# Layer 1 of a two-layer diffusion backbone: v normalised by ScalarE, gates issued behind weight halves, and a rearranged last product

## The chip, the cores and the metric

The kernel runs on one core of a Trainium2 chip. Its time is the device time of one execution in microseconds (us); several runs are made and their median is given. The engines are TensorE (PE, with PEld for its weight loads), VectorE (DVE), ScalarE (ACT), GpSimd (POOL) and SyncE (SP), which only issues transfers here.

## The reference

The model has two layers over 512 latent tokens (width 1024) and 256 context tokens. Layer 0 is a bidirectional retention mixer, and the change leaves it alone. Layer 1, on the latent tokens, is a chunked gMLP:

```
u = h @ w_in[:, :2048];  v = h @ w_in[:, 2048:4096];  z = h @ w_in[:, 4096:]
v = v - mean(v);  v = v * rsqrt(mean(v * v) + eps) * vnorm_g      # per token
mixed = einsum('gij,bnjgc->bnigc', w_s, v in chunks of 128 tokens) + b_s
y = u * mixed
out = (y * silu(z)) @ w_out
x = x + gate * out;   result = rmsnorm(x, final_g)
```

The mean and the square mean run over all 2048 features of a token, so v has to be complete before one value of it can be normalised. Everything is float32; the matmuls are made of three products of a rounded high part and a low part.

## The kernel before, in words

**High and low parts.** Each weight tile of 128 x 1024 is loaded raw by SP, then split: ACT casts it to the high part (`CAST hl<-raw`), DVE subtracts that from the raw tile for the low part (`TENSOR_TENSOR hl<-raw,hl`, called the low below). `mm3` (line 109) issues the three products. One helper (line 54) records every PE, ACT and DVE instruction, so the profile names line 54 for all of them and the tile names tell them apart.

**Seven products for eight.** u and z of layer 1 are made in eight units (i = 0 to 7). A unit takes four raw tiles, named 11, 12, 22 and 21, and forms seven products of a Strassen-like scheme in the order `SINGLE = ("B11", "T1", "T2", "B21", "T3", "B22", "T4")`. A T product first needs a difference of two raw tiles (`TENSOR_TENSOR raw<-raw` on DVE), then cast and low. Each product is 24 matmuls of 256 columns. The four results are 11, 12, 22 and 21; ACT copies (`COPY snap<-pst`) and DVE sums (`TENSOR_TENSOR snap<-pst,snap`) take the first three out of PSUM, the last stays there. B11, T2, T3 and T4 add into one PSUM bank (`Product.run`), so the copy after T2 has to be over before T3 writes.

**Weight halves ahead.** `Q.get()` (class `Stream`, line 137) hands out the next split tile and writes the splitting of the tiles up to two further on into the program. Split tiles live in four rotating buffers (`hl`), raw tiles in seven slots, other temporaries in eleven rotating buffers (`t2`: `snap`, `vt`, `ya`, `yz`, `xs`). SP issues transfers in order; one whose slot is still read holds up those behind it.

**v.** v was made before the units and stored in DRAM as `vt`, one block of 256 features per unit. `load_vt` (line 1266) brings a block back as two tiles and DVE normalises each 128 x 256 piece in place, four per unit. After B22 of a unit 16 small matmuls (`pst<-wsT,vt`) mix the tokens of that block: two banks, one for each of the two feature tiles 2i and 2i+1.

**Gates.** `gate_f` (line 1276) makes y of one feature tile: silu(z) on ACT (`yz`), mixed times norm gain plus bias (`SCALAR_TENSOR_TENSOR ya<-pst,sv,bsb`), two multiplications by u, one by silu(z), then cast and low. Feature tile 2i+1 takes results 12 and 22, feature tile 2i takes 11 and 21, the last of which comes with T4. The first is written behind B22, the second behind T4.

**Last product.** `out1(p)` (line 1211), p = 0 to 3, multiplies four y tiles by the output weights; p = 0, 1, 2 follow units 2, 4, 6, and p = 3 follows unit 7. It works on two column halves (hf) of 512, for each on four row tiles t of 128 tokens, and k runs over the four y tiles; p = 3 ends in `final`, the last RMSNorm and the store of the rows. For p = 3, hf = 0 the y tiles k = 0, 1, 3 come first for each t, and k = 2 (feature tile 14, which waits for T4) last.

**Order.** PE works in the order of the text. In this part of the program ACT, DVE and SP are free within data dependencies: a scheduler of the language sets their order when the program is built, so the order on each engine is fixed but not that of the text.

Of the kernel before, what the change touches and what calls it, by code (L numbers as in the profile page):

```python
# [9 lines left out]
AF = mybir.ActivationFunctionType  # L10
ALU = mybir.AluOpType
AX = mybir.AxisListType

P = 128
D = 1024
# [4 lines left out]
NT = SEQ // P  # L20
# [6 lines left out]
HS = 256  # L27
# [40 lines left out]
def hybrid_kernel(ctx, tc, xT_d, cT_d, cv_d, sv_d, rows_d, ada0_d, adag_d, w_d, rope_d, dec_d, ws_d, id_d, out_d):  # L68
    nc = tc.nc
    pe, act, dve = (Queue(tc, e) for e in (nc.tensor, nc.scalar, nc.vector))  # L70
# [11 lines left out]
    def st(shape, tag, dt=F32, bufs=1, name=None):  # L82
        return sb.tile(shape, dt, tag=tag, name=name or tag, bufs=bufs)

    T2 = 11
# [15 lines left out]
    def t2(name, shape=(P, 512), dt=F32):  # L101
        return st(list(shape), "t2", dt, bufs=T2, name=name)

    def pt(shape=(P, 512), tag="ps"):
        return ps.tile(list(shape), F32, tag=tag, name="pst", bufs=6 if tag == "ps" else 2)
# [3 lines left out]
    def mm3(out, l, r, first, last):  # L109
        (lh, ll), (rh, rl) = l, r  # L110
        mm(out, ll, rh, start=first, stop=False, skip_group_check=True)
        mm(out, lh, rl, start=False, stop=False, skip_group_check=True)
        mm(out, lh, rh, start=False, stop=last, skip_group_check=True)

    def split(hl, src, late=None):
        h, l = hl
        act.copy(h, src)
        low = lambda: dve.tensor_tensor(l, src, f32(h), ALU.subtract)
        if late is None:
            low()  # L120
        else:
            late.append(low)
# [4 lines left out]
    def load(dst, src):  # L127
        nc.sync.dma_start(dst, src)  # L128
# [83 lines left out]
    Q = Stream()  # L212
# [62 lines left out]
    UZ = 8  # L275
# [918 lines left out]
    fg = st([P, D], "g0", name="fg")  # L1194
    load(fg, rows_d[1:2, :].partition_broadcast(P))

    mv = st([P, NT, 2], "mv")
    for t in range(NT):
        dve.bn_aggr(mv[:, t, :], bns[:, t, :, :])
    rv = st([P, NT], "rv")  # L1200
# [3 lines left out]
    o1 = [st([P, D], f"s{t}", name="o1") for t in range(NT)]  # L1204
# [3 lines left out]
    def yf(f):  # L1208
        return ys[f % 6]

    def out1(p):
        for hf in range(2):
            ws = [Q.get() for _ in range(2)]
            pr = {}
            if p == 3 and hf == 0:
                seq = [(t, k) for ks in ((0, 1, 3), (2,)) for t in range(NT) for k in ks]
            else:
                seq = [(t, k) for t in range(NT) for k in range(4)]
            ends = (2,) if p == 3 and hf == 0 else (3,)
            for t, k in seq:  # L1220
                if k == 0:
                    pr[t] = pt()
                y = yf(4 * p + k)
                w = ws[k // 2][:, :, k % 2 * 512:k % 2 * 512 + 512]
                mm3(pr[t], (y[:, 0, t * P:t * P + P], y[:, 1, t * P:t * P + P]), (w[:, 0, :], w[:, 1, :]), k == 0, k in ends)
                if k in ends:
                    drain(p, t, hf, pr.pop(t))

    def drain(p, t, hf, pr):
        h = slice(hf * 512, hf * 512 + 512)  # L1230
        s = o1[t][:, h]
        if p == 0:
            act.copy(s, pr)
            return
        dve.tensor_tensor(s, pr, s, ALU.add)
        if p == 2:
            xs = t2("xs")
            load(xs, x1_d[2 * t + hf])
            dve.tensor_tensor(s, s, Q.gate[:, h], ALU.mult)
            dve.tensor_tensor(s, s, xs, ALU.add)  # L1240
        if p == 3:
            final(t, hf, s, h)

    ends = {}

    def final(t, hf, s, h):
        if hf == 0:
            ends[t] = (st([P, 2], "fss", bufs=4), st([P, D], f"w{t}", name="o"))
        ss, o = ends[t]
        act.activation(t2("junk1"), s, AF.Square, accum_out=ss[:, hf:hf + 1])  # L1250
        if hf == 0:
            dve.tensor_scalar(ss[:, 0:1], ss[:, 0:1], 1.0 / D, EPS, ALU.mult, ALU.add)
        dve.tensor_tensor(o[:, h], s, fg[:, h], ALU.mult)
        if hf == 0:
            return
        rows = out_d[t * P:t * P + P, :]
        act.activation(ss[:, 1:2], ss[:, 1:2], AF.Sqrt, bias=ss[:, 0:1], scale=1.0 / D)
        dve.reciprocal(ss[:, 1:2], ss[:, 1:2])
        dve.tensor_scalar(o[:, 0:512], o[:, 0:512], ss[:, 1:2], None, ALU.mult)
        load(rows[:, 0:512], o[:, 0:512])  # L1260
        act.activation(o[:, 512:], o[:, 512:], AF.Copy, scale=ss[:, 1:2])
        load(rows[:, 512:], o[:, 512:])

    vts = {}

    def load_vt(i):
        vts[i] = []
        for th in range(2):
            v = t2("vt", (P, 2, HS))
            load(v, vt_d[i][:, 2 * th:2 * th + 2, :])  # L1270
            for t in range(2):
                n = 2 * th + t
                dve.tensor_scalar(v[:, t, :], v[:, t, :], mv[:, n, 0:1], rv[:, n:n + 1], ALU.subtract, ALU.mult)
            vts[i].append(v)

    def gate_f(f, pm, mine):

        g = f // 2
        a = t2("ya")
        z1 = t2("yz")  # L1280
        bb = bsb[:, g * P:g * P + P].unsqueeze(1).to_broadcast([P, NT, P])
        for th in range(2):
            act.activation(z1[:, th * HS:th * HS + HS], mine[th][:, HS:], AF.Silu)
        dve.scalar_tensor_tensor(a.rearrange("p (n i) -> p n i", n=NT), pm.rearrange("p (n i) -> p n i", n=NT),
                                 vg[:, f:f + 1], bb, ALU.mult, ALU.add)
        for th in range(2):
            h = a[:, th * HS:th * HS + HS]
            dve.tensor_tensor(h, mine[th][:, 0:HS], h, ALU.mult)
        dve.tensor_tensor(a, a, z1, ALU.mult)
        y = yf(f)  # L1290
        split((y[:, 0, :], y[:, 1, :]), a)

    load_vt(0)
    for i in range(UZ):
        got, pms = {}, {}
        prod = Product(features, got.__setitem__)
        for name in SINGLE:
            prod.run(name, Q.get())
            if name == "T2" and i < UZ - 1:
                load_vt(i + 1)  # L1300
            if name == "B22":
                for s in range(2):
                    pm = pms[s] = pt()
                    for n in range(NT):
                        mm(pm[:, n * P:n * P + P], vts[i][n // 2][:, n % 2, s * P:s * P + P], wsT[:, i * P:i * P + P], start=True, stop=True)
                gate_f(2 * i + 1, pms[1], {0: got["12"], 1: got["22"]})
        gate_f(2 * i, pms[0], {0: got["11"], 1: got["21"]})
        if i and i % 2 == 0:
            out1(i // 2 - 1)
    out1(3)  # L1310


# [108 lines left out]
```

## Time and profile before

| what | value |
|---|---|
| median of 3 runs | 913.14 us (909.51 to 913.16) |
| profiled execution | 911.76 us |
| its span, first to last instruction | 910.0 us |
| PE busy | 886.6 us (97%) |
| DVE busy | 722.4 us (79%) |
| ACT busy | 445.5 us (49%) |
| clock granted to TensorE, mean | 0.997 |

A timeline row gives the start in us, the length in us, the engine, the line, the instruction with its tiles and shape, how many it merges (x24), and in brackets the idle time ahead of it on that engine with what ended it. A row of grouped instructions gives the count, the busy time, the mean length in ns, and the idle time ahead. Instructions of one engine overlap a little, so a merged row is shorter than the count times the mean.

Units 0 to 7 begin on PE at 635.72 us; the last matmul ends at about 903.7 us.

### The profile page before, as it was taken

How to read it: one execution, taken by the hardware profiler on the slowest of the kernel's cores; microseconds unless marked ns; L12 is line 12 of the kernel's file. 1: busy time of each engine (PE TensorE's matmuls, PEld its weight loads, DVE VectorE, ACT ScalarE, POOL GpSimd, SP SyncE). 2: the span in 40 equal slices, each digit the busy share in tenths (PEclk: the TensorE clock that was granted, in tenths of full speed). 3: DMA queues.
4: the chain of work that ended last, by engine and by line, in shares of the span. 5: the costliest groups of instructions: out<-in, count | busy, mean ns of one | idle time of the engine just before them, and what ended most of it. 6: DMA issues, size and time to landing. Idle time of an engine off the chain costs nothing.

```text
span 910.0 us, 16953 instructions
## 1 busy us (share of the span) xinstructions
PE 886.6 (97%) x6872; PEld 840.4 (92%) x6872; DVE 722.4 (79%) x1024; ACT 445.5 (49%) x683; POOL 51.5 (6%) x88
## 2 busy tenths in 40 slices
PE   8999999999999999999999999999999999999987
PEld 6899999999999998998989798999999899899885
DVE  3689978698789866888666759999899479679985
ACT  5565644434545436626362548744546445244244
POOL 0001211101102010000000001111000000000000
PEclk9999999999999999999999999999999999999999
DMA  9943968556667377758163611626335035037102
GB/s 334 389 136 111 308 200 255 163 183 223 211 207 241 107 254 251 257 164 282 43 194 107 200 37 66 200 102 220 129 116 185 24 116 185 24 117 253 49 24 93
DMA packets 76782, 153.81 MB, mean 169 GB/s; under 512 B 7840, under 2 KB 34592, under 8 KB 76704
## 3 DMA queue, kind: packets, MB, share of 16 engines
q1 hardware_dynamic: 69840, 130.70, 44.5%
q0 software_dynamic: 6720, 22.03, 6.3%
q8 instruction: 54, 0.88, 0.4%
q14 instruction: 24, 0.20, 0.1%
q10 hardware_dynamic: 144, 0.01, 0.0%
HBM read 128.58 MB, written 24.12 MB: 168 GB/s over the span
## 4 chain that ended last, share of the span: by engine, by line
PE 61%; DVE 20%; DMA 7%; ACT 5%; issue 5%; SPq 1%; DVEq 0%; ACTq 0%
PE pst L54 61%; DVE hl L54 5%; DMA raw<-in_w_dram 4%; DVE raw L54 4%; DVE ya L54 2%; ACT hl L54 2%; DVE o L54 2%; DMA vt<-vt 2%; SPq L128 1%; DMA acc<-in_xT_dram 1%; DVE pf L54 1%; DMA xq<-in_xT_dram 1%; DVE snap L54 1%; DVE ada_a L54 1%; ACT junk L54 1%
## 5 line engine op out<-in xcount | busy, mean ns | idle before, releaser
L54 DVE TENSOR_TENSOR hl<-raw,hl 128x1024 fp32r<-128x1024 f32 x195 | 236.7, 1222 | 65.5 <-ACT hl L54 64.8
L54 ACT CAST hl<-raw 128x1024 fp32r<-128x1024 f32 x195 | 202.7, 1049 | 140.9 <-DVE raw L54 71.1
L54 PE MATMUL pst<-oS,hl 128*128 128x256 f32 x1104 | 135.6, 280 | 4.3 <-DVE hl L54 3.7
L54 PEld LDWEIGHTS pst<-oS,hl 128*128 128x128 f32 x1104 | 131.4, 188 | 6.6 <-ACT ya L54 3.6
L54 PE MATMUL pst<-hl,oS 128*128 128x256 f32 x1152 | 137.3, 279 | 0.1
L54 PEld LDWEIGHTS pst<-hl,oS 128*128 128x128 f32 x1152 | 135.6, 188 | 1.2 <-ACT snap L54 0.8
L54 PE MATMUL pst<-oA,hl 128*128 128x256 f32 x936 | 118.1, 281 | 0.2
L54 PEld LDWEIGHTS pst<-oA,hl 128*128 128x128 f32 x936 | 112.6, 188 | 2.6 <-DVE raw L54 0.8
L54 DVE TENSOR_TENSOR raw<-raw 128x1024 f32<-128x1024 f32 x92 | 111.5, 1221 | 0.8
L54 PE MATMUL pst<-hl,oA 128*128 128x256 f32 x816 | 99.4, 280 | 0.1
L54 ACT COPY snap<-pst 128x512 f32<-128x512 f32 x92 | 53.9, 586 | 89.4 <-PE pst L54 89.1
L54 PEld LDWEIGHTS pst<-hl,oA 128*128 128x128 f32 x816 | 96.9, 188 | 0.4 <-issue 0.3
L54 PE MATMUL pst<-og,hl 128*128 128x256 f32 x768 | 93.1, 281 | 0.0
L54 PEld LDWEIGHTS pst<-og,hl 128*128 128x128 f32 x768 | 91.2, 188 | 1.0 <-issue 0.5
L54 PE MATMUL pst<-hl,ya 128*128 128x512 f32 x288 | 69.6, 394 | 2.4 <-DVE ya L54 2.4
L54 PEld LDWEIGHTS pst<-hl,ya 128*128 128x128 f32 x288 | 53.9, 188 | 14.7 <-DVE ya L54 2.9
L54 PE MATMUL pst<-v,ph 128*128 128x512 f32 x192 | 60.9, 399 | 0.0
L54 DVE TENSOR_TENSOR snap<-pst,snap 128x512 f32<-128x512 f32 x69 | 47.4, 687 | 4.1 <-PE pst L54 3.9
L54 ACT CAST ph<-pf 128x512 fp32r<-128x512 f32 x24 | 14.9, 621 | 70.9 <-DVE pf L54 68.5
L54 PE MATMUL pst<-hl,hc 128*128 128x256 f32 x384 | 47.5, 279 | 0.0
L54 PEld LDWEIGHTS pst<-hl,hc 128*128 128x128 f32 x384 | 45.9, 188 | 0.0
L54 PEld LDWEIGHTS pst<-v,ph 128*128 128x128 f32 x192 | 36.7, 191 | 7.7
(172 smaller groups left out, 971.8 us busy)
## 6 DMA issues: line engine op xcount, KB each, us to landing
raw<-in_w_dram SPq DMA_DIRECT2D x224, 256.0 KB, 4.5
bg<-in_adag_dram SPq DMA_DIRECT2D x32, 512.0 KB, 4.4
ada_w<-in_ada_dram SPq DMA_DIRECT2D x16, 512.0 KB, 9.0
raw<-in_w_dram SPq DMA_DIRECT2D x16, 512.0 KB, 4.4
bg<-in_dec_dram SPq DMA_DIRECT2D x12, 512.0 KB, 4.3
v<-snap POOLq DMA_DIRECT2D x16, 256.0 KB, 5.1
z<-snap POOLq DMA_DIRECT2D x16, 256.0 KB, 4.7
v<-v SPq DMA_DIRECT2D x8, 512.0 KB, 4.2
```

Of the source, the lines that this page charges most:

```text
L54: made = op(*args, **kw)
L128: nc.sync.dma_start(dst, src)
```

## The change

Four edits, all in layer 1:

- v is normalised by ACT: y = rv * v + nb with nb = -mean * rv, a 128 x 4 tile made once by DVE (`ACTIVATE vt<-vt,nb,rv`), where DVE had subtracted and multiplied. The block for the next unit is now loaded after T1 (it was T2), and its normalisation is written after T4.
- A gate isn't written at once but put on a list (`owed`). `settle`, called after the next `Q.get()`, first pins the DVE order at that point (`fence`: later DVE instructions stay behind the one recorded last) and then writes the gates that are owed. In unit 7 the second gate is written at once.
- In the last product, hf = 0: k = 0 and 1 for all row tiles, then k = 3 for all, then k = 2 for all.
- In the last product, hf = 1: the last row tile is made in two column pieces of 256 (`last`), each with its own sum of squares; the last store is issued by ACT's queue instead of SP's.

```
             ws = [Q.get() for _ in range(2)]
             pr = {}
+            settle()
             if p == 3 and hf == 0:
-                seq = [(t, k) for ks in ((0, 1, 3), (2,)) for t in range(NT) for k in ks]
+                seq = [(t, k) for ks in ((0, 1), (3,), (2,)) for t in range(NT) for k in ks]
...
+                if (p, hf, t) == (3, 1, NT - 1):
+                    continue
...
+            if (p, hf) == (3, 1):
+                t = NT - 1
+                for c in range(2):
+                    pq = pt((P, HS))
+                    for k in range(4):
+                        y = yf(4 * p + k)
+                        o = k % 2 * 512 + c * HS
+                        w = ws[k // 2][:, :, o:o + HS]
+                        mm3(pq, (y[:, 0, t * P:t * P + P], y[:, 1, t * P:t * P + P]), (w[:, 0, :], w[:, 1, :]), k == 0, k == 3)
+                    last(t, c, pq)
...
+    def last(t, c, pq):
+        h = slice(512 + c * HS, 512 + c * HS + HS)
+        s = o1[t][:, h]
+        dve.tensor_tensor(s, pq, s, ALU.add)
+        ss, o = ends[t]
+        act.activation(t2("junk1", (P, HS)), s, AF.Square, accum_out=ss[:, 1:2])
+        dve.tensor_tensor(o[:, h], s, fg[:, h], ALU.mult)
+        if c == 0:
+            dve.scalar_tensor_tensor(ss[:, 0:1], ss[:, 1:2], 1.0 / D, ss[:, 0:1], ALU.mult, ALU.add)
+            return
...
+        act.activation(o[:, 512:], o[:, 512:], AF.Copy, scale=ss[:, 1:2])
+        nc.scalar.dma_start(rows[:, 512:], o[:, 512:])
...
             load(v, vt_d[i][:, 2 * th:2 * th + 2, :])
-            for t in range(2):
-                n = 2 * th + t
-                dve.tensor_scalar(v[:, t, :], v[:, t, :], mv[:, n, 0:1], rv[:, n:n + 1], ALU.subtract, ALU.mult)
             vts[i].append(v)
+    nb = st([P, NT], "nb")
+    dve.scalar_tensor_tensor(nb, mv[:, :, 0], -1.0, rv, ALU.mult, ALU.mult)
+    def norm_vt(i):
+        for n in range(NT):
+            v = vts[i][n // 2][:, n % 2, :]
+            act.activation(v, v, AF.Identity, bias=nb[:, n:n + 1], scale=rv[:, n:n + 1])
+    owed = []
+    def settle():
+        if owed:
+            dve.fence()
+        while owed:
+            owed.pop(0)()
...
     load_vt(0)
+    norm_vt(0)
     for i in range(UZ):
...
         for name in SINGLE:
-            prod.run(name, Q.get())
-            if name == "T2" and i < UZ - 1:
-                load_vt(i + 1)
+            w = Q.get()
+            settle()
+            prod.run(name, w)
+            if i < UZ - 1:
+                if name == "T1":
+                    load_vt(i + 1)
+                if name == "T4":
+                    norm_vt(i + 1)
...
-                gate_f(2 * i + 1, pms[1], {0: got["12"], 1: got["22"]})
-        gate_f(2 * i, pms[0], {0: got["11"], 1: got["21"]})
+                owed.append(lambda f=2 * i + 1, pm=pms[1], mine={0: got["12"], 1: got["22"]}: gate_f(f, pm, mine))
+        owed.append(lambda f=2 * i, pm=pms[0], mine={0: got["11"], 1: got["21"]}: gate_f(f, pm, mine))
+        if i == UZ - 1:
+            settle()
```

How the instructions move is shown at three places; numbers behind names are those of buffers and differ between the two programs. First DVE, where unit 1 ends and the T2 tile of unit 2 is made. Before, `ya_7951` is the gate of feature tile 3, `ya_7989` that of feature tile 2, and `hl_8000<-raw_7594` is the low of the T2 tile:

```order
L54 SCALAR_TENSOR_TENSOR ya_7951<-pst_7946,sv_95,bsb_7460 128x512
L54 SCALAR_TENSOR_TENSOR ya_7989<-pst_7941,sv_95,bsb_7460 128x512
L54 TENSOR_TENSOR ya_7951<-snap_7836,ya_7951 128x256
L54 TENSOR_TENSOR ya_7951<-snap_7803,ya_7951 128x256
L54 TENSOR_TENSOR ya_7989<-snap_7773,ya_7989 128x256
L54 TENSOR_TENSOR ya_7951<-ya_7951,yz_7952 128x512
L54 TENSOR_TENSOR ya_7989<-pst_7748,ya_7989 128x256
L54 TENSOR_TENSOR raw_7594<-raw_7630,raw_7594 128x1024
L54 TENSOR_TENSOR ya_7478<-ya_7951,ya_7478 128x512
L54 TENSOR_TENSOR ya_7989<-ya_7989,yz_7990 128x512
L54 TENSOR_TENSOR hl_8000<-raw_7594,hl_8000 128x1024
L54 TENSOR_TENSOR ya_7478<-ya_7989,ya_7478 128x512
```

The same place in the changed program, where `ya_7953` is feature tile 3, `ya_7995` feature tile 2, and `hl_7992<-raw_7592` the low of the T2 tile; `hl_8032` is the low of B21, the product after it:

```order
L54 TENSOR_TENSOR raw_7592<-raw_7628,raw_7592 128x1024
L54 SCALAR_TENSOR_TENSOR ya_7953<-pst_7944,sv_95,bsb_7460 128x512
L54 TENSOR_TENSOR ya_7953<-snap_7842,ya_7953 128x256
L54 TENSOR_TENSOR ya_7953<-snap_7805,ya_7953 128x256
L54 TENSOR_TENSOR hl_7992<-raw_7592,hl_7992 128x1024
L54 TENSOR_TENSOR ya_7953<-ya_7953,yz_7954 128x512
L54 SCALAR_TENSOR_TENSOR ya_7995<-pst_7939,sv_95,bsb_7460 128x512
L54 TENSOR_TENSOR hl_8032<-raw_7815,hl_8032 128x1024
L54 TENSOR_TENSOR ya_7478<-ya_7953,ya_7478 128x512
L54 TENSOR_TENSOR ya_7995<-snap_7775,ya_7995 128x256
L54 TENSOR_TENSOR ya_7995<-pst_7750,ya_7995 128x256
```

Before, seven gate instructions stood ahead of the raw difference for T2 (`raw<-raw`) and two more between it and its low; now there are three between the two, none ahead, and the rest of the gates follows behind the low.

Second ACT in unit 1, where the block of v for unit 2 (`vt_7807`, `vt_7809`) is normalised. `snap_7842` is the copy out of PSUM after T2, which T3 waits for. Before:

```order
L54 COPY snap_7773<-pst_7748 128x512
L54 CAST ya_7478<-ya_7734 128x512
L54 CAST hl_7775<-raw_7554 128x1024
L54 CAST hl_7806<-raw_7297 128x1024
L54 COPY snap_7803<-pst_7778 128x512
L54 CAST hl_7846<-raw_7300 128x1024
L54 COPY snap_7836<-pst_7748 128x512
L54 CAST hl_7879<-raw_7554 128x1024
```

and in the changed program (`snap_7836` above is `snap_7842` here):

```order
L54 COPY snap_7775<-pst_7750 128x512
L54 CAST hl_7812<-raw_7297 128x1024
L54 CAST ya_7478<-ya_7740 128x512
L54 COPY snap_7805<-pst_7780 128x512
L54 CAST hl_7844<-raw_7300 128x1024
L54 ACTIVATE vt_7807<-vt_7807,nb_7481,rv_7471 128x256
L54 COPY snap_7842<-pst_7750 128x512
L54 CAST hl_7877<-raw_7560 128x1024
L54 ACTIVATE vt_7807<-vt_7807,nb_7481,rv_7471 128x256
L54 ACTIVATE vt_7809<-vt_7809,nb_7481,rv_7471 128x256 x2
```

The first normalisation stands ahead of the copy after T2, so that copy also waits for the transfer of `vt_7807`. The same happens in units 4 and 6; in units 0, 2, 3 and 5 the copy comes first.

Third PE, the end of the program: the last product, one piece of the difference.

```order
 L54 MATMUL pst<-wsT,vt 128x128 x8
 L54 MATMUL pst<-oA_6831,hl 128x256 x24
-L54 MATMUL pst<-hl,ya 128x512 x96
-L1417 UNCONDITIONAL_BRANCH
+L54 MATMUL pst<-hl,ya 128x512 x84
+L54 MATMUL pst<-hl,ya 128x256 x24
+L1470 UNCONDITIONAL_BRANCH
```

Twelve matmuls of 512 columns became 24 of 256.

More of the change, by code (lines that the diff above doesn't have):

```diff
@@ L1262, in final @@
         load(rows[:, 512:], o[:, 512:])
+    def last(t, c, pq):
[8 more added lines that the diff above has]
+            return
+        rows = out_d[t * P:t * P + P, :]
+        act.activation(ss[:, 1:2], ss[:, 1:2], AF.Sqrt, bias=ss[:, 0:1], scale=1.0 / D)
+        dve.reciprocal(ss[:, 1:2], ss[:, 1:2])
+        dve.tensor_scalar(o[:, 0:512], o[:, 0:512], ss[:, 1:2], None, ALU.mult)
+        load(rows[:, 0:512], o[:, 0:512])
+        act.activation(o[:, 512:], o[:, 512:], AF.Copy, scale=ss[:, 1:2])
+        nc.scalar.dma_start(rows[:, 512:], o[:, 512:])
     vts = {}
```

## The prediction

> **What bounds the kernel now.** I read the page's shares first, then TensorE's timeline over layer 1, then DVE's timeline at one of TensorE's gaps, and last the end of the program. The page:
>
> ```profile
> span 910.0 us, 16953 instructions
> PE 886.6 (97%) x6872; PEld 840.4 (92%) x6872; DVE 722.4 (79%) x1024; ACT 445.5 (49%) x683; POOL 51.5 (6%) x88
> ```
>
> TensorE is busy for 97%, and the change takes no matmul work away. It can only gain where TensorE stands still behind 635 us, and behind the last matmul. TensorE's timeline of units 0 to 7 has five gaps:
>
> ```profile
> 663.90 3.04 PE L54 MATMUL pst<-oS,hl 128*128 128x256 f32 x24 [0.94 <-DVE hl L54]
> 687.21 3.04 PE L54 MATMUL pst<-oS,hl 128*128 128x256 f32 x24 [1.60 <-DVE hl L54]
> 690.09 2.96 PE L54 MATMUL pst<-oA,hl 128*128 128x256 f32 x24
> 752.82 3.04 PE L54 MATMUL pst<-oS,hl 128*128 128x256 f32 x24 [0.56 <-DVE hl L54]
> 819.02 3.04 PE L54 MATMUL pst<-oS,hl 128*128 128x256 f32 x24 [0.62 <-DVE hl L54]
> 878.84 1.56 PE L54 MATMUL pst<-hl,ya 128*128 128x512 f32 x6
> 882.83 20.88 PE L54 MATMUL pst<-hl,ya 128*128 128x512 f32 x90 [2.43 <-DVE ya L54]
> ```
>
> The first four are T2 of units 1, 2, 4 and 6, each waiting for a low; they sum to 0.94 + 1.60 + 0.56 + 0.62 = 3.72 us. The fifth is the last product waiting for a y tile, 2.43 us. What lies ahead of the largest of the four, on DVE:
>
> ```profile
> 680.20 1.40 DVE L54 SCALAR_TENSOR_TENSOR ya<-pst,sv,bsb 128x512 f32<-128x512 f32 x2
> 681.51 1.08 DVE L54 TENSOR_TENSOR ya<-snap,ya 128x256 f32<-128x256 f32 x3
> 682.52 0.69 DVE L54 TENSOR_TENSOR ya<-ya,yz 128x512 f32<-128x512 f32 x1
> 683.12 0.42 DVE L54 TENSOR_TENSOR ya<-pst,ya 128x256 f32<-128x256 f32 x1
> 683.45 1.22 DVE L54 TENSOR_TENSOR raw<-raw 128x1024 f32<-128x1024 f32 x1
> 684.59 0.69 DVE L54 TENSOR_TENSOR ya<-ya 128x512 fp32r<-128x512 f32 x1
> 685.19 0.69 DVE L54 TENSOR_TENSOR ya<-ya,yz 128x512 f32<-128x512 f32 x1
> 685.84 1.23 DVE L54 TENSOR_TENSOR hl<-raw,hl 128x1024 fp32r<-128x1024 f32 x1
> ```
>
> DVE has no idle time here: two gates run, and the low that TensorE waits for ends at 687.07. In units 0 and 1 DVE is close to full, 18.80 of 20 us:
>
> ```profile
> 680.00:700.00 20.00, 18.40 (x158) 18.23 (x157) 18.80 (x27) 11.48 (x15) 0.00 (x0) 1.00 0.43 136
> 840.00:860.00 20.00, 20.00 (x98) 16.69 (x97) 20.00 (x30) 3.73 (x5) 0.00 (x0) 1.00 0.24 91
> ```
>
> (columns: stretch, length, busy PE, PEld, DVE, ACT, POOL, granted clock, transfer share, GB/s). ACT has room in both.
>
> **The change part by part.** First v on ACT. What DVE loses and ACT gains:
>
> ```profile
> L54 DVE TENSOR_SCALAR vt<-vt,mv,rv 128x256 f32<-128x256 f32 x32 | 11.5, 411 | 11.1 <-DMA vt<-vt 11.0
> L54 ACT ACTIVATE f<-f,sh,gs 128x256 f32<-128x256 f32 x16 | 8.3, 592 | 1.1 <-DVE f L54 1.1
> L54 ACT ACTIVATE yz<-snap 128x256 f32<-128x256 f32 x24 | 9.2, 413 | 27.5 <-DVE snap L54 27.4
> ```
>
> DVE is rid of 11.5 us of work and of 11.1 us spent standing behind `vt` transfers, 2.8 us a unit. The new ACT instruction is the form of the second row, an earlier scaling with a column of scales and one of shifts: 0.59 us; the nearest cheaper row, 0.41, is the lower end. ACT gains 32 x 0.59 = 18.9 us (13.2 by the lower end), 2.4 a unit, and in units 0 and 1 it is busy for 11.48 of 20 us. No part of this is on TensorE's path by itself. [...]
>
> Second the gates behind weight halves. Ahead of the low at 685.84 the new order leaves one `SCALAR_TENSOR_TENSOR` (half of 1.31), two `ya<-snap` (two thirds of 1.01) and the raw difference; the other gate work, from 680.20 to 685.84 without the raw difference 4.50 us, shrinks to 0.66 + 0.67 = 1.33. So the low comes 3.2 us earlier by the order alone, and by up to 2.8 us more from v: twice and more the largest gap of 1.60. I take all four gaps as gone, **3.72 us**; the lower bound is 0, where the raw tiles and not DVE set the time (rival A). What becomes late instead is the second gate of each unit. Its y tile is needed at the earliest after the next unit but for the last product, and its two PSUM banks return six allocations later, so nothing waits for it up to unit 6.
>
> At unit 7 there is a cost. The second gate of unit 6 now lies between the row sums of the last but one product, where the second windows row shows DVE at 20.00 of 20 us. T2's raw difference of unit 7 now stands behind nearly all those sums. Counting the new order from the end of unit 6's T4 with the lengths above and 0.6 us for each 512-column row operation, its low ends some 0.3 us after T2 could start. I take **-0.3 us**, with 0 to -1.
>
> Third the order of the last product. Six matmuls took 878.84 to 880.24; now the 24 of k = 0 and 1 take 4 x 1.40 = 5.6 us, so tile 15 is needed at 884.4 and tile 14 at 884.4 + 2.8 = 887.2. In the profile the lows of both ended by 883.4:
>
> ```profile
> 879.89 0.42 DVE L54 TENSOR_TENSOR ya<-pst,ya 128x256 f32<-128x256 f32 x1
> 880.95 1.22 DVE L54 TENSOR_TENSOR hl<-raw,hl 128x1024 fp32r<-128x1024 f32 x1
> 882.08 1.29 DVE L54 TENSOR_TENSOR ya<-ya 128x512 fp32r<-128x512 f32 x2
> ```
>
> By the new order tile 15 is done ahead of them and tile 14 about 2 us later, some 885.4. Either way the gap closes, **2.43 us**. The new wait is that of the fourth row tile's PSUM bank, which is freed when T4's result has been multiplied in; it starts 4.2 us behind T4, at 883.0, and needs an operation that ended at 880.3 and may come 1.6 us later.
>
> Fourth the end. From the last matmul on it is a chain on DVE and ACT (the first two rows are steps of earlier row tiles, for their lengths):
>
> ```profile
> 895.77 0.15 DVE L54 TENSOR_SCALAR fss<-fss 128x1 f32<-128x1 f32 x1
> 903.31 0.49 DVE L54 TENSOR_SCALAR o<-o,fss 128x512 f32<-128x512 f32 x1
> 903.74 0.69 DVE L54 TENSOR_TENSOR o<-pst,o 128x512 f32<-128x512 f32 x1
> 904.47 0.63 ACT L54 ACTIVATE junk<-o 128x512 f32<-128x512 f32 x1 [0.43 <-DVE o L54]
> 905.22 0.29 ACT L54 ACTIVATE fss<-fss 128x1 f32<-128x1 f32 x1
> 905.75 0.72 ACT L54 ACTIVATE o<-o,fss 128x512 f32<-128x512 f32 x1 [0.23 <-DVE fss L54]
> 906.69 0.38 SPq L128 DMA_DIRECT2D out_dram<-o  x1
> ```
>
> TensorE does the same columns: 24 of 256 take 2.8 us (from 687.21 to 690.09, and a little less without the start), 12 of 512 also 2.8 (twice 1.40). The last addition falls from 0.69 to 0.42 (the `ya<-pst` row), the square by some 0.2. Against that, DVE has the first piece's and the third row tile's steps in front (0.49 and 0.15 us), which delay the addition by about 0.2. The last store was issued at 906.69, 0.22 after its data were ready at 906.47, behind SP's other store; ACT issues it at once. That is 0.27 + 0.2 - 0.2 + 0.2, about **0.5 us**, with 0 (all of the first piece's steps in the way) to 0.7 (none). [...]
>
> **Sum.** 3.72 + 2.43 + 0.5 - 0.3 = 6.35 us. The profiled execution took 911.76, 1.76 more than its span, so 905.4. It stands 1.38 under the median of 913.14, from which the same sum gives 906.8. I say 906. A measurement of this kernel can tell about 0.5%, 4.6 us, from no change, so the gain is not far above what can be seen.
>
> **Rivals.**
>
> A, the raw tiles set the time. DVE asks earlier, but a raw tile only comes when its slot is free. For: the chain of waits in unit 1 has
>
> ```profile
> 672.54 3.52 DMA raw<-in_w_dram
> 676.07 1.23 DVE raw L54
> ```
>
> so the raw difference began just as its tile landed. Against: DVE's whole wait for raw tiles, 640 to 910 us, is
>
> ```profile
> DVE raw L54 <- DMA raw<-in_w_dram: 0.4, 2, 0.3
> ```
>
> 0.4 us in two places, and slots come free earlier as well. Then the four gaps stay: 911.76 - 2.43 - 0.5 + 0.3 = 909.1.
>
> B, slower: ACT stands behind a late `vt`. In units 1, 4 and 6 the first normalisation is ahead of the copy after T2, which T3 needs, and SP may load the block only when the gate of the unit before has read its first snapshot. That read ended here:
>
> ```profile
> 658.20 1.09 DVE L54 TENSOR_TENSOR ya<-snap,ya 128x256 f32<-128x256 f32 x3
> L128 SPq DMA_DIRECT2D vt<-vt x16: 326/379/433, 622.9 to 823.4; - x16
> DMA to landing us min/median/max: 2.3/4.2/6.5
> 669.59 5.76 PE L54 MATMUL pst<-oS,hl 128*128 128x256 f32 x48
> ```
>
> Now a low, a multiplication, a raw difference and a y low come ahead of the read (1.14 + 0.6 + 1.14 + 0.6), so it ends near 662.7. The block lands at 666.9 (665 to 669.2), its first normalisation and the copy take 0.59 + 0.59: 668.1. T3, without the gap, starts at 669.59 - 0.94 = 668.65. That holds by 0.6 us at the median and fails by 1.7 at the longest landing. The kernel turns slower when the three copies are late by more than 6.35 / 3 = 2.1 us each, with the load's start 0.4 us later still and the longest landing. At 3.5 us each it is 905.4 + 10.5 = 915.9. Against: units 4 and 6 follow a stage where DVE catches up, and every landing would have to be long.
>
> C, the fence and the scheduler bring the gaps back elsewhere, at T1 or B21 behind a gate, with nothing won but the end: 911.3.
>
> **How the numbers follow.** Forecast 0.64, A 0.20, B 0.08, C 0.08. The forecast's own range is 903 to 909: 6.35 off the lowest run of 909.51 gives 903.2, off 913.14 it gives 906.8, and one long landing (1.7) 908.5. The range over the cases is 903 to 911.5: it takes in A and C and leaves out B and the ends. Faster by over 0.5% needs more than 4.6 of the 6.35 us: the forecast less a tenth for a missed gap or a different run, and a little of A, 0.60. Within 0.5%: A, C and that tenth, 0.32. Slower: B, 0.08.
>
> **What would show it.** Right: TensorE's timeline has no gap over 0.3 us ahead of T2 in units 1, 2, 4 and 6 and none in the last product; DVE's busy time falls by some 11 us and its wait for `vt` is gone; ACT's rises by 13 to 19; the last store is issued about 2.5 us behind the last matmul (3.0 before). Wrong: gaps with `raw<-in_w_dram` as what ended DVE's wait (A), ACT idle ahead of `vt<-vt,nb,rv` with TensorE waiting for `ACT snap` at T3 of units 1, 4 and 6 (B), or gaps at other products (C).

## The result and the profile after

| kernel | median | range of the runs | profiled execution | its span |
|---|---|---|---|---|
| before, first comparison | 912.77 us (17 runs) | 909.51 to 916.78 | 911.76 | 910.0 |
| changed | 904.39 us (17 runs) | 901.08 to 910.28 | 908.63 | 906.8 |
| before, second comparison | 911.78 us (15 runs) | 909.10 to 914.66 | | |
| changed, once more | 903.58 us (6 runs) | 901.26 to 904.41 | 904.26 | 902.5 |

The ratio is 0.9913 with a 95% interval of 0.9896 to 0.9929 in the first comparison, and 0.9908 (0.9892 to 0.9924) in the second. Of 912.77 that is 7.9 us less (6.5 to 9.5). 906 was forecast, 1.6 us more than the median, which lies in the range (903 to 911.5); the sum behind it was a gain of 6.35 us.

The profiled execution of the changed kernel is one of its longer ones. The page of after:

```profile
span 906.8 us, 16974 instructions
PE 887.9 (98%) x6884; PEld 843.6 (93%) x6884; DVE 715.0 (79%) x996; ACT 460.2 (51%) x717; POOL 51.5 (6%) x88
```

Its span is only 3.2 us shorter than that of before, because it lost 4.4 us ahead of the change: unit 0 begins on TensorE at 640.09 us where it began at 635.72, in a part of the program that is the same in both. The last section shows where. So the two profiles are compared from a landmark inside the stage, the small matmuls of unit 0's gate, up to the last matmul. The first two rows are TensorE's timeline of before, the other two that of after:

```profile
652.53 1.95 PE L54 MATMUL pst<-wsT,vt 128*128 128x128 f32 x16
894.61 9.09 PE L54 MATMUL pst<-hl,ya 128*128 128x512 f32 x39
```

```profile
656.90 1.95 PE L54 MATMUL pst<-wsT,vt 128*128 128x128 f32 x16
894.82 6.02 PE L54 MATMUL pst<-hl,ya 128*128 128x512 f32 x37
```

From 652.53 to 903.70 are 251.2 us, from 656.90 to 900.84 they are 243.9: 7.2 us gained. (The second profile of the changed kernel has 244.5 there, 6.7 us less than before.) From the last matmul to the end of the span it was 6.3 us and is 5.95, another 0.3.

Where the 7.2 us were is seen best in the timeline of TensorE's weight loads (PEld), which has the same five gaps as the matmuls, longer by 0.17 to 0.18 us at T2 and by 0.43 in the last product, since the profile models the ends of matmuls. The releaser in the brackets of its rows isn't always the last one: at 687.18 the cast named there had ended 0.26 us ahead of the low that TensorE's own row names. All its idle times behind 600 us, before:

```profile
663.87 2.87 PEld L54 LDWEIGHTS pst<-oS,hl 128*128 128x128 f32 x24 [1.12 <-ACT ya L54]
687.18 2.87 PEld L54 LDWEIGHTS pst<-oS,hl 128*128 128x128 f32 x24 [1.77 <-ACT ya L54]
752.79 2.87 PEld L54 LDWEIGHTS pst<-oS,hl 128*128 128x128 f32 x24 [0.73 <-ACT ya L54]
818.99 2.87 PEld L54 LDWEIGHTS pst<-oS,hl 128*128 128x128 f32 x24 [0.80 <-ACT yb L54]
882.82 20.45 PEld L54 LDWEIGHTS pst<-hl,ya 128*128 128x128 f32 x90 [2.86 <-DVE ya L54]
```

and after, with the last product below it:

```profile
862.25 2.89 PEld L54 LDWEIGHTS pst<-oS,hl 128*128 128x128 f32 x24 [0.59 <-DVE hl L54]
```

```profile
878.26 22.59 PE L54 MATMUL pst<-hl,ya 128*128 128x512 f32 x108
```

Of 7.28 us of waiting, 0.59 is left. It is T2 of unit 7, a place that had no gap before. The last product runs through in one piece.

That makes 6.7 us. The other 0.5 is a difference of pace: 96 matmuls of `out1` take 22.57 us in some passes and 22.15 in others, at a granted clock of 1.00 in both. In the profile of before p = 1 and p = 2 took 22.57 and in that of after 22.15 (together 0.8 us), while the last product of after took 22.59 where the same matmuls take 22.23 in three other kernels below. The pass p = 1 was slow in the three kernels that leave the units as they were (before, order alone, last rows alone) and fast in all the others. What sets the pace was not tried.

### The profile page after: what moved, and what is told of

The parts are those of the page before. It is cut to its first block, busy times and chain, and to the rows that moved or that the text cites. A ratio compares the mean times of both kernels' runs of the same rounds, so it can differ in the third digit from the quotient of the medians.

```text
span 906.8 us, 16974 instructions
## 1 busy us (share of the span) xinstructions
PE 887.9 (98%) x6884; PEld 843.6 (93%) x6884; DVE 715.0 (79%) x996; ACT 460.2 (51%) x717; POOL 51.5 (6%) x88
## 4 chain that ended last, share of the span: by engine, by line
PE 80%; DVE 9%; DMA 4%; ACT 4%; issue 2%; SPq 1%; DVEq 0%; ACTq 0%
PE pst L54 80%; DVE hl L54 2%; DVE o L54 2%; DMA acc<-in_xT_dram 1%; DMA raw<-in_w_dram 1%; DVE raw L54 1%; DMA xq<-in_xT_dram 1%; ACT hl L54 1%; DVE pf L54 1%; SPq L128 1%; ACT f L54 1%; DVE ya L54 1%; ACT junk L54 1%; DVE pl L54 0%; ACT ph L54 0%
## 5 line engine op out<-in xcount | busy, mean ns | idle before, releaser
L54 PE MATMUL pst<-hl,ya 128*128 128x512 f32 (+1 forms) x300 | 69.3, 384 | 0.0
L54 PEld LDWEIGHTS pst<-hl,ya 128*128 128x128 f32 x300 | 54.7, 188 | 11.5
```

Source lines behind the costliest of these rows:

```text
L54: made = op(*args, **kw)
```

## The experiments

The question was which of the four edits does what, and why the gain is somewhat larger than the sum. The theory of the prediction: the low of T2 is late because DVE's queue ahead of it holds a gate and v's pieces that stand behind their transfers; both edits together bring it forward, and the new order closes the fifth gap. The rivals: one of the two edits is enough and the other idle; raw tiles set the time; ScalarE becomes the late engine. The sizes below come from several comparisons, each kernel against runs of the kernel before on the same chip.

| kernel | median (runs) | ratio to before, 95% | waits of PEld behind 600 us |
|---|---|---|---|
| v on ScalarE alone | 908.71 (10) | 0.9968 (0.9949 to 0.9987) | 2.62 |
| the same, again | 907.60 (9) | 0.9960 (0.9944 to 0.9976) | 2.61 |
| gates behind weight halves alone | 911.08 (10) | 0.9985 (0.9962 to 1.0007) | 0.21 + 0.26 + 1.24 + 0.34 + 0.80 + 2.51 |
| order of the last product alone | 907.27 (1) | one run | 1.21 + 0.88 + 0.59 + 0.65 |
| last rows in pieces alone | 916.32 (1) | one run | 1.33 + 0.87 + 0.29 + 3.33 |
| changed without the gate list | 904.51 (6) | 0.9915 (0.9887 to 0.9943) | none |
| changed without the new order | 903.71 (6) | 0.9911 (0.9884 to 0.9939) | 0.59 |
| v on ScalarE, fifth wait filled | 906.46 (11) | 0.9936 (0.9917 to 0.9956) | none |
| the same, again | 905.84 (7) | 0.9942 (0.9920 to 0.9965) | none |
| changed, v passed through ScalarE twice | 908.12 (1) | one run | 0.59 |
| changed, last store on SP | 903.95 (6) | 0.9921 (0.9903 to 0.9939) | 0.59 |

**v on ScalarE alone.** The edit:

```
-            for t in range(2):
-                dve.tensor_scalar(v[:, t, :], v[:, t, :], mv[:, n, 0:1], rv[:, n:n + 1], ALU.subtract, ALU.mult)
+    def norm_vt(i):  (as in the change; load_vt(i + 1) behind T1, norm_vt(i + 1) behind T4)
```

> The kernel before with only the first edit: v normalised by ACT, its block loaded after T1; gates, last product and last rows as before. Theory (two covers that overlap: either the DVE time freed or the new order alone is more than the gaps): DVE is freed of 2.8 us a unit, more than the largest gap, so TensorE's four gaps at T2 of units 1, 2, 4 and 6 (weight loads idle 1.12, 1.77, 0.73, 0.80 us before) shrink to under 0.3 us each; the gap of 2.86 us in the last product stays between 2 and 3; the end stays at 6.3 us behind the last matmul. Time some 4.4 us less than before. Rival (the order of gates and lows is what counts): at least half of the 4.4 us of gaps is left. Second rival (ACT becomes the bound): new gaps at T3 behind the copy after T2.

The four gaps at T2 are gone with this edit alone; the weight loads have one idle time left, the fifth:

```profile
878.12 22.02 PEld L54 LDWEIGHTS pst<-hl,ya 128*128 128x128 f32 x90 [2.62 <-DVE ya L54]
```

So it was v that made the low late, by its 11.5 us of work on DVE or by the 11.0 us that DVE stood behind `vt`. Three profiles tell which: the kernel before and the two kernels below with the third or the fourth edit alone have the same units and the same order on DVE there, but their `vt` transfers landed at different times. The waits are those of DVE's timeline, as here in unit 1 of before, 0.71 + 1.25 = 1.96 us:

```profile
671.69 0.74 DVE L54 TENSOR_SCALAR vt<-vt,mv,rv 128x256 f32<-128x256 f32 x2 [0.71 <-DMA vt<-vt]
673.68 0.73 DVE L54 TENSOR_SCALAR vt<-vt,mv,rv 128x256 f32<-128x256 f32 x2 [1.25 <-DMA vt<-vt]
```

| T2 of unit | DVE's wait for `vt` in the unit ahead (before, order alone, last rows alone), us | wait of PEld at T2, us |
|---|---|---|
| 1 | 1.88, 1.93, 2.14 | 1.12, 1.21, 1.33 |
| 2 | 1.96, 1.08, 1.07 | 1.77, 0.88, 0.87 |
| 4 | 1.34, 1.31, 0.77 | 0.73, 0.59, none |
| 6 | 1.47, 1.31, 0.90 | 0.80, 0.65, 0.29 |

Each gap follows the wait for `vt` ahead of it, to within 0.2 us, and is shorter than that wait: by these rows none of the four would have been there without the waits. The waits in units 2, 4 and 6, of up to 2.00 us, left no gap; a pass of `out1` lies between them and the next T2. Whether less work on DVE alone, or the earlier load alone (behind T1, also part of this edit), would do as much was not tried.

In time the edit gave 2.9 us (1.2 to 4.7), and 3.6 (2.2 to 5.1) in a second comparison; 4.4 us of gaps had gone, which both intervals hold. The clock was lowered behind the wait that was left, which the runs further down take up.

**Gates behind weight halves alone.** The edit is `owed` and `settle`, with v left on DVE:

```
+            w = Q.get()
+            settle()
+            prod.run(name, w)
-                gate_f(2 * i + 1, ...)
+                owed.append(lambda ...: gate_f(...))
```

> The kernel before with only the second edit: gates put behind the next weight halves; v stays on DVE and is loaded after T2, last product and last rows as before. Theory (overlapping covers): the low ahead of T2 comes about 3 us earlier by the order alone, so the four gaps shrink to under 0.3 us each, the gap in the last product stays between 2 and 3 us, and T2 of unit 7 shows a gap of some 0.4 us as in the changed kernel. Time some 4 us less than before. Rival (the freed DVE time is what counts): DVE still stands behind the transfers of v for some 11 us and at least half of the 4.4 us of gaps is left.

The gaps don't go; they move, much as rival C had it for the whole change, but to T3 and T4, and some is left at T2. The largest in units 0 to 6 is now at T3 of unit 2, and a still larger one stands at T2 of unit 7. In the first row below the weight loads name ScalarE's copy, but that had ended at 691.55 and the low, which TensorE's own row (the second) names, at 691.88, so DVE is late here too:

```profile
691.99 5.72 PEld L54 LDWEIGHTS pst<-oS,hl 128*128 128x128 f32 x48 [1.24 <-ACT snap L54]
692.02 5.89 PE L54 MATMUL pst<-oS,hl 128*128 128x256 f32 x48 [1.07 <-DVE hl L54]
863.39 4.04 PEld L54 LDWEIGHTS pst<-oS,hl 128*128 128x128 f32 x24 [2.51 <-DVE hl L54]
```

DVE still stands behind the `vt` transfers, 11.9 us in nine waits (from its waits, 630 to 910 us: total, number, longest), and what follows in its fixed order stands there with it:

```profile
DVE vt L54 <- DMA vt<-vt: 11.9, 9, 2.3
```

The fifth gap is gone here, with the old order of the last product. By time the edit alone can't be told from no change.

**Order of the last product alone.**

```
-                seq = [(t, k) for ks in ((0, 1, 3), (2,)) for t in range(NT) for k in ks]
+                seq = [(t, k) for ks in ((0, 1), (3,), (2,)) for t in range(NT) for k in ks]
```

> The kernel before with only the third edit: k = 0 and 1 for all row tiles first, then 3, then 2. Theory: the four gaps at T2 stay as before (4.4 us of idle weight loads in all, each within 0.3 us), the gap in the last product goes from 2.86 us to under 0.2, and unit 0 to the last matmul takes 2.9 us less than the 268.0 us before. Rival (the wait moves to the PSUM bank of the fourth row tile): a gap of 1 us or more is left in the last product.

The fifth gap closes. The four at T2 stay, but not at their size: they sum to 3.33 us, and T2 of unit 2 has 0.88 where 1.77 was expected, since DVE waited less for `vt` in this execution (table above). The last product:

```profile
877.05 22.15 PE L54 MATMUL pst<-hl,ya 128*128 128x512 f32 x96
```

**Last rows in pieces alone.** The edit is the `last` part of the diff.

> The kernel before with only the fourth edit: last row tile in two column pieces, last store issued by ACT's queue. Theory: the five gaps stay; from the last matmul to the end it takes 5.9 to 6.0 us as in the changed kernel, where it was 6.3, so 0.3 us of gain. Rival (the first piece's steps cost what the second saves): 6.2 to 6.4 us.

Four of the five waits are there (none at T2 of unit 4), the fifth of 3.33 us, and this one execution was a long one. The edit can only be read in the tail: from the last matmul to the end of the span 6.1 us, where kernels without this edit have 6.23 to 6.32 in seven profiles and the others with it 5.93 to 6.06 in six. The edit is worth about 0.3 us.

**The change without the gate list.** Edits one, three and four; the gates are written at once as before.

```
-            settle()
-            w = Q.get()
-            settle()
-            prod.run(name, w)
+            prod.run(name, Q.get())
-                owed.append(lambda ...: gate_f(...))
+                gate_f(2 * i + 1, ...)
```

> The changed kernel without its second edit: v on ACT, order of the last product and last rows as changed, but gates issued at once as in the kernel before. In the run of the first edit alone TensorE had no gap at T2 at all, and in the run of the third alone none in the last product. Theory now (v on ACT pays for the four gaps, the order of the last product for the fifth, and the list of gates adds nothing in this company): no gap over 0.3 us in units 0 to 7 and in the last product, T2 of unit 7 included (0.59 us of idle weight loads in the changed kernel), ratio to the kernel before 0.989 to 0.993. Rival (the list is needed once DVE is less loaded as well): gaps of 0.5 us or more at T2 come back, or the last product waits, ratio 0.994 or more.

Same time as the changed kernel within the intervals, and no wait at all in the weight loads behind 600 us, not even the 0.59 at T2 of unit 7. The last product:

```profile
875.54 22.23 PE L54 MATMUL pst<-hl,ya 128*128 128x512 f32 x108
```

**The change without the new order.** Edits one, two and four; the `seq` line is that of before.

> The changed kernel without its third edit: the last product keeps k = 0, 1, 3 and then 2. In the run of the second edit alone the gap in the last product was gone with the old order. Theory (two covers for the fifth gap, either is enough): no gap over 0.5 us in the last product, ratio 0.989 to 0.993, not to be told from the changed kernel. Rival (the new order is needed): a gap of 1 us or more there, and, if it is over some 2 us, a granted clock under 0.9 in the 5 us behind it.

Again the same time, and no fifth gap; the 0.59 at T2 of unit 7 stays:

```profile
858.07 2.87 PEld L54 LDWEIGHTS pst<-oS,hl 128*128 128x128 f32 x24 [0.59 <-DVE hl L54]
874.01 22.23 PE L54 MATMUL pst<-hl,ya 128*128 128x512 f32 x108
```

DVE's timeline shows how the list does it. With v on ScalarE alone the two last gates are interleaved and the lows of their y tiles come together, in the last of the rows:

```profile
872.25 1.40 DVE L54 SCALAR_TENSOR_TENSOR ya<-pst,sv,bsb 128x512 f32<-128x512 f32 x2
...
876.24 1.22 DVE L54 TENSOR_TENSOR hl<-raw,hl 128x1024 fp32r<-128x1024 f32 x1
877.38 1.29 DVE L54 TENSOR_TENSOR ya<-ya 128x512 fp32r<-128x512 f32 x2
```

With the list, here without the new order, the gate of tile 15 goes first and its low is done before the other gate begins:

```profile
874.39 0.69 DVE L54 TENSOR_TENSOR ya<-ya 128x512 fp32r<-128x512 f32 x1 [0.69 <-ACT ya L54]
875.00 0.74 DVE L54 SCALAR_TENSOR_TENSOR ya<-pst,sv,bsb 128x512 f32<-128x512 f32 x1
```

The last product began at 874.38 in the one and at 874.01 in the other and needs tile 15 some 1.4 us later, near 875.8 and 875.4. The first of the two lows from 877.38 on ends at 878.1, the low from 874.39 at 875.1. So the second and the third edit close the same gap, and one of them is idle in the changed kernel. Which of the two is dropped makes no difference that these runs can tell.

**v passed through ScalarE twice.** This asks how much room ScalarE has, which rival B denied. Each normalised piece goes through one more `ACTIVATE` that multiplies by one and adds zero.

```
             act.activation(v, v, AF.Identity, bias=nb[:, n:n + 1], scale=rv[:, n:n + 1])
+            act.activation(v, v, AF.Identity, bias=cpad[:, 0, 2:3], scale=ones[:, 0:1])
```

> The changed kernel with every piece of v run through ACT a second time (scale one, shift zero), so ACT does 32 more instructions of 0.59 us, 2.4 us a unit. Theory (ACT has room for the moved work): TensorE's gaps in units 0 to 7 stay under 0.6 us each, unit 0 to the last matmul 244 to 245 us from the first small matmuls on, as in the changed kernel (243.95). Rival (ACT was nearly full with v): gaps at T3 behind the copies after T2, 1 us or more in units 1, 4 and 6.

ScalarE's groups, 630 to 910 us:

```profile
L54 ACT ACTIVATE vt<-vt,nb,rv 128x256 f32<-128x256 f32 x32 | 17.8, 592 | 2.0 <-DMA vt<-vt 2.0
L54 ACT ACTIVATE vt<-vt,cpad,ones 128x256 f32<-128x256 f32 x32 | 18.2, 595 | 0.1
```

With 18.2 us more on ScalarE no further wait of TensorE appears. The stretch from the small matmuls to the last matmul is 244.5 us; the changed kernel has 243.9 and 244.5 in its two profiles. The 908.12 of the one run comes from ahead of this stage. One thing the run does not test: in unit 1 all pieces stand behind the copy that T3 needs here, and in units 4 and 6 the one piece ahead of the copy has its second pass behind it, so no piece in front of the copy was doubled.

**The fifth wait filled.** The first edit alone gave, by its medians, less than the gaps that it removed, and its profile showed a lowered clock behind the wait that was left. To take the wait away without changing its cause, TensorE is given 12 matmuls of a constant tile there, whose result nobody reads (the profile counts 24, two for each):

```
+                if (p, hf, t, k) == (3, 0, 0, 3):
+                    idle = pt((P, P), tag="tm")
+                    for _ in range(12):
+                        mm(idle, ones, ones, start=True, stop=True, skip_group_check=True)
```

> The kernel with the first edit alone, and 12 matmuls of ones with ones (128 x 128, about 0.2 us each) put on TensorE where the last product waits for tile 15; they write a bank that nobody reads. In the run without them the wait was 2.6 us, the granted clock 0.82 in the 5 us behind it, and the last 90 matmuls took 22.46 us against 20.88 in the kernel before. Theory (a gap costs more than its length, since the clock is lowered behind it): the clock stays at 1.00 from 870 us on, the last 90 matmuls take under 21.2 us, mean clock of the runs 0.997 or more where it was 0.995 to 0.996, median 1 to 2 us under that of the first edit alone (908.7). Rival (the clock drop there was chance, or follows from something else): the 90 matmuls take 22 us or more, the same median.

It was faster than the first edit alone, by 0.0032 in the ratio, but in another comparison. So both were put on one chip, with the changed kernel:

> The first edit alone, once more, so that it stands on one chip beside the filled wait and the changed kernel. It left one wait of TensorE's weight loads, 2.62 us in the last product, and behind that wait the profile showed the granted clock at 0.92 in 870 to 880 and 0.82 in 880 to 885, with the last 90 matmuls 22.46 us long against 20.88 in the kernel before. Theory: the wait costs its own 2.6 us and, in most executions, 1 to 2 us of lowered clock behind it; then this kernel takes about 909 us, 1 to 2.5 us more than the kernel with the wait filled. Rival: the lowered clock was chance and would have come anyway; then the two take the same time, within 0.6 us.

> The first edit, with 12 matmuls of a constant tile in the wait of the last product, whose result nobody reads. They took 2.84 us for a wait of 2.62 us, so by their own length they gain nothing (+0.3 us). Theory: the granted clock stays at 1.00 up to the end of the last product, and the kernel takes 1 to 2.5 us less than the first edit alone, about 907 us. Rival: within 0.6 us of the first edit alone, or slower.

> The changed kernel on the same chip. It has no wait to fill in the last product: against the kernel with the wait filled it saves 2.6 us of filling and 0.3 us at the end, and pays 0.6 us at T2 of unit 7: 2.4 us less by either theory. Against the first edit alone the theory has 3.4 to 4.9 us less, the rival 2.4 us less.

The last product's matmuls with the wait, v on ScalarE alone (second profile), and the stretch behind the wait in the table by stage (the column behind POOL's is the granted clock):

```profile
878.88 22.35 PE L54 MATMUL pst<-hl,ya 128*128 128x512 f32 x90 [2.19 <-DVE ya L54]
880.00:885.00 5.00, 5.00 (x19) 4.04 (x18) 0.00 (x0) 0.00 (x0) 0.00 (x0) 0.79 0.00 0
```

and with the wait filled (second profile):

```profile
878.67 2.84 PE L54 MATMUL pst<-ones 128*128 128x128 f32 x24
881.27 20.86 PE L54 MATMUL pst<-hl,ya 128*128 128x512 f32 x90
880.00:885.00 5.00, 5.00 (x30) 4.36 (x29) 1.57 (x3) 0.00 (x0) 0.00 (x0) 1.00 0.01 3
```

The same 90 matmuls take 22.46 and 22.35 us behind the wait, 20.86 both times behind the filling. The times go the same way: 907.60 against 905.84, a ratio lower by 0.0018, and by 0.0032 in the first pair; each difference alone is uncertain by some 0.0028, the mean of both, 0.0025 with about 0.0019 to each side, is 2.3 us (0.5 to 4.1). The traces show 1.5 less 0.2 that the filling is longer than the wait. So the filling, which does no useful work, makes the kernel faster. The changed kernel lies 2.3 us under the filled one (903.58 against 905.84) and 4.0 under the first edit alone; 2.4 and 3.4 to 4.9 were expected by the theory, 2.4 for the second by the rival. A difference of such medians is uncertain by some 2 us, so the 4.0 doesn't decide between them.

**The last store on SP.** One line, in `last`:

```
-        nc.scalar.dma_start(rows[:, 512:], o[:, 512:])
+        load(rows[:, 512:], o[:, 512:])
```

> The changed kernel with its last store issued by SP's queue, as in the kernel before, and not by ScalarE's. In the profile of the changed kernel ScalarE issued it 0.03 us behind its data, in 0.35 us, and the span ended 3.47 us after; in the kernel before SP's store ended the span 3.31 us after it was issued. If the queue matters, SP's earlier piece of the row tile is ahead of this store and it ends 0.1 to 0.6 us later; if only the landing matters, it ends 0 to 0.2 us earlier. Both are less than these rounds can tell; the tail of the profile (last matmul to the end of the span, 5.95 us in the changed kernel) decides.

From the last matmul to the end of the span it is 6.02 us with SP and 5.99 with ScalarE's queue in the profile of the same comparison. ScalarE issues the store earlier, 2.48 us behind the last matmul where SP issues it after 2.73, but from the issue to the end it is 3.51 us with ScalarE and 3.29 with SP. The queue of this store makes no difference in these profiles, so the 0.3 us of the fourth edit are left for the halved last steps.

## Why the prediction came out right, point by point

**What bounds the kernel** held. TensorE's five gaps were all there was to win in layer 1, and the gain from landmark to landmark (7.2 us) is their sum of 7.28, less the 0.59 of unit 7, and 0.5 us of `out1`'s pace. One reading was of the wrong place, without harm: the row of 680 to 700 us, taken for units 0 and 1, is unit 2; in 640 to 660 and 660 to 680 DVE was busy for 17.43 and 17.84 of 20 us.

**The four gaps, 3.72 forecast.** All gone, as forecast, and worth 4.42 in the weight loads. The term was sized on TensorE's modelled idle time, which is 0.2 us shorter at each gap than that of the weight loads. The reason given was half right. The prediction credited the order of the gates with 3.2 us of the low's advance and v with up to 2.8; by the runs v alone is enough, and the order alone leaves or moves the gaps, to T2, T3, T4 and unit 7. What was named second, as "up to 2.8 us more", was the cause, so the size came out right on a reason that was the smaller half of the argument. It is also the size in one execution: with the same units it was 4.42, 3.33 and 2.49 us in three profiles.

**The price on ScalarE, no term in the sum.** Held: TensorE's weight loads have one wait behind 600 us, the 0.59 us of unit 7, and it is for DVE. One piece takes 595 ns where 592 was taken. ScalarE's groups after, 630 to 910 us:

```profile
L54 ACT ACTIVATE vt<-vt,nb,rv 128x256 f32<-128x256 f32 x32 | 17.6, 595 | 2.0 <-DMA vt<-vt 1.9
```

The busy time of ScalarE rose by 14.7 us (445.5 to 460.2; 13 to 19 forecast). DVE's fell by 7.4, where 11 was forecast. The lengths of its instructions add up to 12.6 us less (785.6 to 773.0): 32 pieces of 0.41 us are gone, some small ones are new. But busy time counts the overlap of neighbours once, and there is less of that in the changed kernel (63.2 to 58.0 us).

**Unit 7, -0.3 forecast.** The right place and sign; 0.59 measured. Without the gate list it is zero, so the list is its cause. The way is the prediction's too: with the list DVE's next raw difference starts at 858.10, behind nearly all row sums, and the low after it ends at 862.2, where T2 starts at 862.25; without the list that raw difference starts at 853.61, between the row sums. No gate stands among them.

**The fifth gap, 2.43 forecast.** Closed, 2.86 in the weight loads. The new order does it, but so does the gate list alone. The prediction saw that the list brings tile 15 forward ("done ahead of them"), but not that this would be enough, and put the whole term down to the order of the last product.

**The end, 0.5 forecast.** 0.3. Of the four parts the 0.2 for the store's queue was wrong: the last store was issued 2.48 us behind the last matmul, as forecast, 0.03 behind its data, but the span ended 3.47 us later instead of 3.31, and with SP's queue the end is the same. What the earlier issue saved was lost behind it.

```profile
902.58 0.72 ACT L54 ACTIVATE o<-o,fss 128x512 f32<-128x512 f32 x1 [0.23 <-DVE fss L54]
903.33 0.35 ACTq L1294 DMA_DIRECT2D out_dram<-o  x1
```

The second issuing engine was seen at the issue (0.03 us behind the data, 0.22 with SP before the change) and not at the end.

**The sum.** With the measured sizes it is 4.42 + 2.86 - 0.59 + 0.3 = 7.0 us, and 7.9 were measured (6.5 to 9.5). The four sizes make up 0.65 of the 1.55 us that the forecast of 6.35 was short. The other 0.9 needs no cause: 7.0 lies within the interval. Two things that the sum left out point the same way; their share in the medians isn't known. The slower pace of `out1` cost 0.4 us a pass in the profile of before. And the wait of the last product can be followed by a lowered clock, which costs 1.5 us where it comes; it came in both profiles of the first edit and behind the 3.33 us wait of the last rows alone, and not in the profile of before, so the sum made from that profile could not hold it.

**The rivals.** A (raw tiles) fell: DVE, now early, waited 1.0 us for raw tiles, and mostly for ScalarE's casts instead; its wait for `vt` is gone. From DVE's waits after, 630 to 910 us:

```profile
DVE hl L54 <- ACT hl L54: 33.6, 32, 4.8
DVE hl L54 <- DMA raw<-in_w_dram: 1.0, 2, 0.6
```

B (ScalarE behind a late `vt`) fell by a margin of 1.1 us, in unit 1, where the prediction had worked out 0.6. After, in ScalarE's timeline, the piece and the copy; in TensorE's, T3:

```profile
670.62 0.59 ACT L54 ACTIVATE vt<-vt,nb,rv 128x256 f32<-128x256 f32 x1
671.12 0.57 ACT L54 COPY snap<-pst 128x512 f32<-128x512 f32 x1
```

```profile
672.82 2.40 PE L54 MATMUL pst<-oS,hl 128*128 128x256 f32 x19
```

The copy ends at 671.69, T3 starts at 672.82; in units 4 and 6 the margin is 1.9 and 1.5 us. C (the gaps come back elsewhere) did not happen to the change, but is much what the gate list does by itself, at T3, T4 and T2 of unit 7 instead of T1 or B21.

## What to carry to other kernels

When a late operation stands behind two kinds of work in an engine's fixed order, look first for the one that itself waits: each gap here was as long as the wait for a transfer ahead of it made it, to within 0.2 us. Moving the pieces that stood behind transfers to an engine with room took all four away (4.42 us), while reordering the rest around them only moved the waits. A gap that hangs on a transfer also has another size in the next execution (the four summed to 4.42, 3.33 and 2.49 us), so one profile sizes it roughly. Read TensorE's waits from its weight loads, and count a wait of 2.1 us or more as more than its length: in these traces the clock dropped behind most of those, and in the last product the drop cost 1.5 us. Edits that close the same gap don't add: try each with the other left out, and keep the cheaper one.

## What the runs showed of the hardware

That the clock drops behind a wait of TensorE (0.79 in 880 to 885 us behind 2.61 us, 1.00 with the wait filled) was not in the prediction. A place that all kernels share shows it first: in layer 0, at 348 to 350 us, TensorE waits for `pf` from DVE, for a time that differs from one execution to the next. The wait of the weight loads there, and the granted clock in the stretch from 350 to 355 us, one profile each:

| wait, us | granted clock, 350 to 355 us |
|---|---|
| 1.56, 1.61, 1.63, 1.65, 1.95, 2.03 | 1.00 in all six |
| 2.12 | 0.74 |
| 2.43 | 0.70 |
| 2.74, 2.88 | 0.72, 0.75 |
| 3.01, 3.38, 3.59 | 0.66 in all three |
| 3.96 | 0.50 |

The ends of the jump, from the changed kernel again (1.63) and from the second profile with the filled wait (3.96):

```profile
347.80 1.46 PEld L54 LDWEIGHTS pst<-qk 128*128 128x128 f32 x12 [1.63 <-DVE pf L54]
350.00:355.00 5.00, 5.00 (x30) 4.33 (x29) 4.27 (x7) 3.14 (x4) 0.00 (x0) 1.00 0.34 81
```

```profile
349.93 2.64 PEld L54 LDWEIGHTS pst<-qk 128*128 128x128 f32 x12 [3.96 <-DVE pf L54]
350.00:355.00 5.00, 5.00 (x18) 4.52 (x19) 4.27 (x6) 2.79 (x5) 0.00 (x0) 0.50 0.33 104
```

Read in slices of 1 us, the drops are alike: the clock goes down to 0.50, and what it lacks to 1.00 adds up to 1.70 or 1.71 us each time, which is 3.4 us at half clock. With the wait of 3.96 us it is 3.41, twice as much; 0.7 of it lies ahead of 350 us (0.93 in 340 to 350), where the wait ends. The table's values differ because the 5 us slice holds the 3.4 us, or only a part of them.

The length of the wait does not decide alone. At a second place that all kernels share, near 520 us, the weight loads wait for `pl` from DVE:

| wait, us | what the clock lacks to 1.00, us |
|---|---|
| 2.35 to 2.37, in eleven profiles | none in four, 1.7 in three, 3.4 in four |
| 2.28 | 1.7 |
| 1.98, 2.22 | none in both |

The profile of before and that of after have 2.36 us each, ending at 521.95 and 525.05; the clock lacks 1.71 us from 523 us on in the one, and 3.42 from 524 us on, where the wait still runs, in the other.

In layer 1 the clock was lowered behind waits of 2.62 us (0.82 in 880 to 885), 2.61 (0.79), 2.51 at T2 of unit 7 with the gate list alone (0.67 in 865 to 870) and 3.33 (0.66 in 885 to 890), by 1.7 us each; it stayed at 1.00 behind all waits of up to 1.77 us and behind the 2.86 us in the profile of before. So no drop came behind 2.03 us or less in these profiles, and from 2.12 us on it came behind most waits, not all. What lets equal waits end differently no trace here shows.

The two places in layer 0 are also what made the profiled execution of the changed kernel a long one. At the first it waited 3.01 us and lost 1.7 us of clock, against 1.61 us and none in the profile of before; at the second it lost 3.4 us of clock against 1.7. That is 4.8 us for the 4.4 by which unit 0 began later. What makes `pf` late by up to 2.4 us from one execution to the next was not tried.
